# Gate and up of the first 512 columns interleaved per k-unit, quadrants evacuated when complete, down k-units reordered: a Hymba-style block on one Trainium2 core

## The chip, the cores and the metric

The kernel runs on one core of a Trainium2 chip. The metric is the device time of one execution in microseconds (us). Before the change it is 1779.33 us, the median of three executions (1777.89 to 1781.35).

## The reference

The reference is one layer over 256 tokens with D = 2048 and FF = 5632, all in fp32:

```
x = x + 0.5 * swiglu(rms_norm(x, ffn1_norm), w_gate, w_up, w_down)     # ffn1
z = rms_norm(x, mix_norm) @ w_in                                       # 2048 x 5120
y = concat(rms_norm(lru branch of z), rms_norm(short conv branch of z))
x = x + y @ w_out                                                      # the mixer
x = x + 0.5 * swiglu(rms_norm(x, ffn2_norm), ...)                      # ffn2
return rms_norm(x, final_norm)
swiglu(x) = (silu(x @ w_gate) * (x @ w_up)) @ w_down                   # 2048 -> 5632 -> 2048
```

The two swiglu blocks hold most of the work: six weight matrices of 46 MB each.

## The kernel before

**Split products.** [...] A weight unit is 512 rows (a k-unit) by 512 columns, 1 MB. `load` (L155) fetches it from HBM by SyncE's queue (SP) into a raw buffer; `parts_of` (L169) makes hi by two casts on ScalarE (ACT) and lo = raw - hi by one subtraction on VectorE (DVE). `multiply` (L194) then issues 24 matmuls for the 256 tokens (two tiles of 128 tokens, four blocks of 128 rows, three products): first the 16 with the weight's hi, then the 8 with its lo.

**Buffers.** Raw units go through a pool of three buffers. Two further buffers, with the tag "kept", belong to the ffn: a raw unit that is needed for long gets one of those. hi and lo units go through two buffers each, every third one through a further one. [...]

**The norm.** `Norm.turn` (L220) transposes x by PE and writes the gain-scaled result, split, to xT; `squares` sums the squares, `factor` (L237) makes the factor r of each token, and `rows` (L243) spreads r along the free axis by two small matmuls into a bank called pb, copied by DVE to a tile bc.

**The ffn** (`ffn`, L384, called with tag 1 and tag 2). FF is cut into 11 blocks of 512 columns. The first block is done plainly: the gate product over four k-units (in ffn1 by `opening`, L542, with its instructions pinned to the written order, since x has just come from HBM; in ffn2 by `product`, L286), then `norm.factor` and `norm.rows`, and then the up product over the four k-units. Both use the x that is not normalised and apply r behind the sum. Beside the up product DVE and ACT normalise x: per k-unit u, v = hi + lo of xT (`vs`: two tiles v_0 and v_1 with the tag "kept", each for two k-units), v times bc, and v split into the tile x_u; after u = 1 `seven_of` (L308) makes from v_0 four combinations (spare and the quarters of v_0), split into the tiles xs.

The other ten blocks are done two at a time by `seven` (L326), once for gate and once for up: two of the four k-units (rows) by two column blocks by two token tiles are eight products of 128 x 512 x 512, which a scheme of Strassen's kind does with seven, in the banks a, c, e, d; the other two k-units are added plainly (`usual`). The combinations of weights (w11, w12, w22, w21) are made in place by subtractions on DVE (2.29 us each). w11 and w12, needed the longest, are loaded to "kept" buffers:

```python
w11, w12 = get(r0, 0, True), get(r0, 1, True)
```

So in the first `seven` of each ffn these two loads take the buffers of v_0 and v_1. `snap` copies a bank to SBUF by ACT, and four additions at the end of `seven` put the quadrants together; the caller then applies silu or multiplies by the gate.

**The hidden units.** A finished quarter h of 128 tokens x 512 goes on the list `waiting`; `settle` takes it off and calls `turn_hidden` (L397), which transposes it by PE (bank ph), splits it to `hidden[u]` and, where asked, copies the transposed quarter back for `seven_of`. `settle` is called inside the next `seven` of the gate or behind the first k-unit of the down product.

**Down** (`down`, L460, after s = 0, 2 and 4): the hidden units collected so far are multiplied with w_down. Of the four blocks of 512 output columns, blocks 0 and 3 are done by `product`, 1 and 2 together by `seven` with the last two units as its rows; `update` adds half of each to xres. In the product of block 0 the units come in the order of `us`, so the unit m = us[-2] comes before n = us[-1].

The engines run their instructions in the order of the built program; where the program isn't pinned, a scheduler sets that order from the dependencies.

Of the kernel before, what the change touches and what calls it, by code (L numbers as in the profile page):

```python
# [12 lines left out]
AF = mybir.ActivationFunctionType  # L13
ALU = mybir.AluOpType
# [34 lines left out]
def hybrid_block(ctx: ExitStack, tc: tile.TileContext, a: dict, out: bass.AP):  # L49
# [273 lines left out]
    def quad(tile):  # L323
        return tile.rearrange("p (j c) -> p j c", j=UK)

    def seven(w, rows, c0, sf, xs, name, keep, between=None):  # L326


        a, c, e, d = (bank(f"ps_{name}_{n}") for n in "aced")

        def get(u, n, kept=False):
            src = w[u * UK * P : (u + 1) * UK * P, c0 + n * CW : c0 + (n + 1) * CW]
            return load(src, f"{name}_{u}{n}", kept=kept)

        (r0, r1), two = rows, len(xs) > 1
# [6 lines left out]
        def snap(ps, n):  # L342
            s = keep(f"{n}_{name}")
            act.copy(s, ps)
            return s
# [36 lines left out]
        return {(1, 1): u3, (0, 1): u2, (1, 0): a, (0, 0): s1}  # L382

    def ffn(tag, norm, after, opening=None):  # L384
        with tc.tile_pool(name=f"ffn{tag}", bufs=1) as fp:
            extra.append(fp)
            turn_of["hold"] = True
# [27 lines left out]
                    turn_hidden(*waiting.pop(0))  # L415


            if opening:
                Engine.pinned = True
                pg = opening(wg)  # L420
                Engine.pinned = False
                flush()
            else:
                pg = product(wg, 0, range(4), norm.xT.__getitem__, f"g{tag}_0")
                flush()
            norm.factor()
            norm.rows()
            sg = [keep(f"sg{tag}_0_{t}") for t in range(NT)]
            for t in range(NT):
                act.activation(sg[t], pg[t], AF.Silu, scale=norm.r[:, t : t + 1])  # L430
# [4 lines left out]
            bcs = norm.bc.unsqueeze(1).to_broadcast([P, UK, S])  # L435
            xs = []
            for u in range(4):
                x = f32(norm.xT[u])
                dve.tensor_tensor(vs[u], x[:, :, :S], x[:, :, S:], op=ALU.add)
                dve.tensor_tensor(vs[u], vs[u], bcs, op=ALU.mult)  # L440
                xs.append(big(f"x{tag}_{u}"))
                act.copy(xs[u][:, :, :S], vs[u])
                dve.tensor_tensor(xs[u][:, :, S:], vs[u], f32(xs[u][:, :, :S]), op=ALU.subtract)
                if u == 1:
                    pair = [big(f"xs{tag}_{i}") for i in range(2)]
                    sf = seven_of(
                        xs[0], xs[1], {(t, i): vs[i][:, :, t * P : (t + 1) * P] for t in range(NT) for i in range(2)},
                        quad(keep(f"spare{tag}")),
                        [(b[:, :, o : o + P], b[:, :, o + P : o + S]) for b in pair for o in (0, S)],
                    )  # L450
            xs = list(enumerate(xs))[2:]
            pu = product(wu, 0, range(4), norm.xT.__getitem__, f"u{tag}_0")
            for t in range(NT):
                dve.scalar_tensor_tensor(sg[t], pu[t], norm.r[:, t : t + 1], sg[t], op0=ALU.mult, op1=ALU.mult)
                waiting.append((0, t, sg[t], False))
            turn_of["hold"] = False
            if tag == 1:
                prepare()

            def down(last):  # L460
                us = sorted(set(hidden) | {w[0] for w in waiting})

                def update(c, t, ps):
                    xr = xres[:, t, c * CW : (c + 1) * CW]
                    Engine.pinned = last and tag == 2 and c == NC_D - 1
                    dve.scalar_tensor_tensor(xr, ps, 0.5, xr, op0=ALU.mult, op1=ALU.add)
                    if last:
                        after(c, t)

                for c in (0, 3):  # L470
                    end = last and tag == 2 and c == NC_D - 1
                    ps = product(
                        wd, c, us, hidden.get, f"d{tag}_{us[0]}_{c}", end, (lambda i: settle()) if c == 0 else None
                    )
                    for t in range(NT):
                        update(c, t, ps[t])
                    if c == 0:
                        m, n = us[-2:]
# [6 lines left out]
                        q = seven(wd, (m, n), CW, sh, [(u, hidden[u]) for u in us[:-2]], f"d{tag}_{m}", keep)  # L485
                        for c1 in (1, 2):
                            for t in range(NT):
                                update(c1, t, q[t, c1 - 1])
                hidden.clear()
                turned.clear()  # L490

            for s in range(5):
                c0 = CW + 2 * s * CW
                g = seven(wg, (0, 1), c0, sf, xs, f"g{tag}_{s}", keep, settle)
                for q in ((1, 1), (0, 1), (1, 0), (0, 0)):
                    if q == (1, 0):
                        z = keep(f"z{tag}_{s}")
                        act.activation(z, g[q], AF.Silu)
                        g[q] = z
                    else:  # L500
                        act.activation(g[q], g[q], AF.Silu)
                h = seven(wu, (0, 1), c0, sf, xs, f"u{tag}_{s}", keep)
                for t, n in ((1, 1), (0, 1), (1, 0), (0, 0)):
                    dve.tensor_tensor(g[t, n], h[t, n], g[t, n], op=ALU.mult)
                    waiting.append((1 + 2 * s + n, t, g[t, n], s % 2 == 0))
                if s % 2 == 0:
                    down(s == 4)
            extra.clear()
# [30 lines left out]

    n1 = Norm("n1", vec["ffn1_norm"])  # L540

    def opening(wg):  # L542

        ps = [bank(f"ps_g1_0_{t}") for t in range(NT)]
        for u in range(KD // UK):
            src = wg[u * UK * P : (u + 1) * UK * P, :CW]
            if u == 0:
                pieces = ((0, 1), (1, 2), (2, 4))
                raw = load(src, "g1_0_0", pieces, lambda i: load_x(1) if i == 1 else None)
                blk = parts_of(raw, "g1_0_0", pieces, lambda i: n1.turn((i,) if i < 2 else (2, 3)))  # L550
            else:
                blk = unit(src, f"g1_0_{u}")
            for j in range(UK):
                begin, end = u == 0 and j == 0, u == KD // UK - 1 and j == UK - 1
                for t in range(NT):
                    yh, yl = stationary(n1.xT[u], t)[j]
                    pe.matmul(ps[t], yh, blk[j][0], start=begin, stop=False)
                    pe.matmul(ps[t], yl, blk[j][0], start=False, stop=False)
                    pe.matmul(ps[t], yh, blk[j][1], start=False, stop=end)
                if j == (u > 0) and u + 1 < NC_D:  # L560
                    if u:
                        load_x(u + 1)
                        n1.squares(u - 1)
                    n1.turn(range(4 * u + 4, 4 * u + 8))
                elif j == 2 and u + 1 == NC_D:
                    n1.squares(u - 1)
                    n1.squares(u)
        return ps

    held = {}  # L570

    def to_mixer(c, t):
# [3 lines left out]
        else:  # L576
            held["nm"].later(c)

    ffn(1, n1, to_mixer, opening)
    nm = held["nm"]  # L580


# [296 lines left out]
```

## Time and profile before

| | |
|---|---|
| median of three executions | 1779.33 us (1777.89 to 1781.35) |
| the profiled execution's own time | 1779.27 us |
| its span, first to last instruction | 1777.3 us |
| mean granted clock of TensorE | 0.994 |
| PE busy | 1744.6 us, 98% |
| DVE busy | 1494.4 us, 84% |
| ACT busy | 1046.8 us, 59% |
| read from HBM | 339.82 MB, 192 GB/s over the span |

A line of the profile that begins with L42 is an instruction recorded by the kernel's own helper, so all of PE, DVE and ACT stand at L42 and are told apart by their tiles. Tiles are named without buffer numbers and without the ffn's tag: ps_g is the bank of the first gate product, ps_u of the first up product, ps_g_a, ps_g_c and so on the banks of a `seven`; raw, hi and lo with _g, _u, _d are a weight's parts for gate, up and down, with _p those of one of the seven products and with _x those of a `usual` one; ph is a transposed h, pb_n the norm's small matmuls. In a timeline each line has the start, the duration, the engine and operation, output <- inputs, the shapes, and in brackets how long the engine was idle before it and which instruction released it. In the list of waits each line has the engine and tile that waited, what it waited for, the sum, the number of times and the longest.

### The profile page before, as it was taken

The numbers are of one execution on the slowest core, as the hardware profiler recorded it, in microseconds if no ns is written. First come the engines' busy times: TensorE is split into PE (matmuls) and PEld (weight loads), VectorE is DVE, ScalarE is ACT, GpSimd is POOL, SyncE is SP. The second block draws the span as 40 slices with busy tenths as digits, with TensorE's granted clock in tenths as the row PEclk, the third lists the DMA queues.
The fourth block names the chain that finished last, engine by engine and source line by source line (L and its number), as shares of the span: only waits on it lengthen the run. The fifth ranks groups of instructions, "written<-read, shape, count | busy, mean of one in ns | idle before, by whom it ended". The sixth has DMA issues, their size and how long they took to land. (4 is left out here: it accounts for less than half of the span.)

```text
span 1777.3 us, 20302 instructions
## 1 busy us (share of the span) xinstructions
PE 1744.6 (98%) x8031; PEld 1441.5 (81%) x8031; DVE 1494.4 (84%) x1221; ACT 1046.8 (59%) x1342; POOL 6.9 (0%) x32
## 2 busy tenths in 40 slices
PE   7999999999999999999999999999999999999998
PEld 5787888888888888888888887887888888888886
DVE  6898989989789888688987667989899887899895
ACT  6565556656465656575765554656566664556664
POOL 1000000000000000000000000000000000000000
PEclk9999999999999999999999999999999999999999
DMA  7366655574566574456565655574566637555743
GB/s 249 132 214 212 213 189 190 190 245 155 186 196 209 172 256 166 145 188 196 175 196 170 209 189 190 190 242 157 192 214 202 209 135 259 189 190 190 257 158 106
DMA packets 173905, 343.24 MB, mean 193 GB/s; under 512 B 5621, under 2 KB 8049, under 8 KB 173681
## 3 DMA queue, kind: packets, MB, share of 16 engines
q1 hardware_dynamic: 173344, 340.82, 57.2%
q8 instruction: 63, 1.03, 0.2%
q10 hardware_dynamic: 144, 1.05, 0.2%
q14 instruction: 34, 0.27, 0.0%
q0 software_dynamic: 320, 0.07, 0.0%
HBM read 339.82 MB, written 2.10 MB: 192 GB/s over the span
## 5 line engine op out<-in xcount | busy, mean ns | idle before, releaser
L42 PE MATMUL ps_in<-xT_nm,hi_in 128*128 128x512 f32 x640 | 224.1, 395 | 0.0
L42 ACT CAST hi_g_p<-raw_g 128x1024 fp32r<-128x1024 f32 x140 | 140.5, 1048 | 123.4 <-DVE raw_g L42 40.9
L42 DVE TENSOR_TENSOR lo_g_p<-raw_g,hi_g_p 128x2048 fp32r<-128x2048 f32 x70 | 159.7, 2287 | 36.0 <-ACT hi_g_p L42 35.5
L42 ACT CAST hi_u_p<-raw_u 128x1024 fp32r<-128x1024 f32 x140 | 141.5, 1049 | 66.3 <-PE ps_u_a L42 25.9
L42 PE MATMUL ps_in<-xT_nm,lo_in 128*128 128x256 f32 x640 | 178.6, 281 | 0.6 <-DVE lo_in L42 0.6
L42 DVE TENSOR_TENSOR lo_u_p<-raw_u,hi_u_p 128x2048 fp32r<-128x2048 f32 x70 | 159.2, 2286 | 22.2 <-ACT hi_u_p L42 22.1
L42 PE MATMUL ps_d<-hi_d,h 128*128 128x512 f32 x704 | 172.2, 396 | 2.8 <-DVE h L42 2.2
L42 PEld LDWEIGHTS ps_d<-hi_d,h 128*128 128x128 f32 x704 | 132.6, 189 | 33.3 <-DVE h L42 3.0
L42 PEld LDWEIGHTS ps_in<-xT_nm,hi_in 128*128 128x128 f32 x640 | 119.8, 187 | 27.1
L42 ACT CAST hi_d<-raw_d 128x1024 fp32r<-128x1024 f32 x88 | 88.0, 1048 | 81.9 <-PE ps_u_d L42 25.3
L42 DVE TENSOR_TENSOR lo_d<-raw_d,hi_d 128x2048 fp32r<-128x2048 f32 x44 | 100.7, 2289 | 31.7 <-ACT hi_d L42 31.7
L42 PEld LDWEIGHTS ps_in<-xT_nm,lo_in 128*128 128x128 f32 x640 | 120.6, 189 | 1.4 <-DVE lo_in L42 1.1
L42 DVE TENSOR_TENSOR lo_in<-raw_in,hi_in 128x2048 fp32r<-128x2048 f32 x40 | 91.4, 2285 | 32.7 <-ACT hi_in L42 32.5
L42 ACT CAST hi_in<-raw_in 128x1024 fp32r<-128x1024 f32 x80 | 81.5, 1049 | 62.1 <-PE ps_in L42 48.8
L42 ACT CAST hi_d_p<-raw_d 128x1024 fp32r<-128x1024 f32 x84 | 84.5, 1048 | 48.2 <-DVE raw_d L42 21.0
L42 DVE TENSOR_TENSOR lo_d_p<-raw_d,hi_d_p 128x2048 fp32r<-128x2048 f32 x42 | 95.5, 2287 | 18.9 <-ACT hi_d_p L42 18.8
L42 ACT CAST hi_g_x<-raw_g 128x1024 fp32r<-128x1024 f32 x80 | 80.8, 1049 | 41.2 <-PE ps_g_c L42 19.9
L42 ACT CAST hi_u_x<-raw_u 128x1024 fp32r<-128x1024 f32 x80 | 80.6, 1049 | 37.3 <-PE ps_u_c L42 25.8
L42 DVE TENSOR_TENSOR raw_u<-raw_u,raw_u 128x2048 f32<-128x2048 f32 x40 | 91.6, 2291 | 9.4 <-DMA raw_u<-in_ffn_w_up_dram 8.7
L42 DVE TENSOR_TENSOR raw_g<-raw_g,raw_g 128x2048 f32<-128x2048 f32 x40 | 91.5, 2287 | 6.4 <-DMA raw_g<-in_ffn_w_gate_dram 5.8
L42 DVE TENSOR_TENSOR lo_g_x<-raw_g,hi_g_x 128x2048 fp32r<-128x2048 f32 x40 | 91.4, 2286 | 3.8 <-ACT hi_g_x L42 3.7
L42 DVE TENSOR_TENSOR lo_u_x<-raw_u,hi_u_x 128x2048 fp32r<-128x2048 f32 x40 | 91.5, 2287 | 3.7 <-ACT hi_u_x L42 3.1
(349 smaller groups left out, 3612.5 us busy)
## 6 DMA issues: line engine op xcount, KB each, us to landing
raw_u<-in_ffn_w_up_dram SPq DMA_DIRECT2D x88, 1024.0 KB, 5.3
raw_d<-in_ffn_w_down_dram SPq DMA_DIRECT2D x88, 1024.0 KB, 5.1
raw_g<-in_ffn_w_gate_dram SPq DMA_DIRECT2D x87, 1024.0 KB, 5.3
raw_in<-in_w_in_dram SPq DMA_DIRECT2D x40, 1024.0 KB, 5.1
raw_o<-in_w_out_dram SPq DMA_DIRECT2D x16, 1024.0 KB, 5.1
xres<-in_x_dram SPq DMA_DIRECT2D x4, 512.0 KB, 8.3
fin<-in_final_norm_dram ACTq DMA_DIRECT2D x1, 1024.0 KB, 4.7
out_dram<-xres SPq DMA_DIRECT2D x4, 256.0 KB, 2.7
```

Source lines behind the costliest of these rows:

```text
L42: ins = getattr(self.engine, name)(*args, **kwargs)
```

## The change

1. The gate and up products of the first 512 columns are done in one loop: for each k-unit its gate part, then its up part, into four banks. `opening` goes; its pinned order is kept in ffn1 for the first two k-units. Inside that loop `norm.factor` comes after up's k-unit 2 (ffn1) or gate's k-unit 2 (ffn2), and `norm.rows` with the first of the normalising after gate's k-unit 3 (ffn1) or up's k-unit 2 (ffn2). silu of the first block and the multiplication by up follow the loop.
2. `seven` takes a callback `done`, and calls it for each quadrant as soon as its last product is issued: (1,1) after product 6, (0,1) after product 2, (1,0) after the last plain product, (0,0) at the end. The callbacks add the parts (`total`) and apply silu (`gate`) or multiply (`up`); in the down product each part is added to xres by an operation of its own. `between` is called before product 5 instead of after its snap.
3. The up callback calls `settle` at quadrant (1,0), so the two quarters of the unit n are transposed before the last product of up. In the product of block 0 and 3 of down the unit n comes before m, and in down's `seven` the two column blocks change places.

In the built program the pb matmuls come after seven of the eight k-unit parts in ffn1 (24 matmuls of the block are left then) and after six in ffn2 (48 are left); before, they came after the four gate parts (96 are left). The number of matmuls is the same. v_0, v_1 and the first w11, w12 have the same two buffers as before.

```diff
-    def seven(w, rows, c0, sf, xs, name, keep, between=None):
+    def seven(w, rows, cols, sf, xs, name, keep, done, between=None):
...
         product_of(4, w11, c, True)
         s5 = snap(c, "s5")
         usual(0, b2, 1, (e, 1, True, not two), (c, 0, False, False))
+        if between:
+            between()
         dve.tensor_tensor(w11, w22, w11, op=ALU.subtract)
         product_of(5, w11, a)
         u2 = snap(a, "u2")
-        if between:
-            between()
...
         product_of(6, w12, a)
         u3 = snap(a, "u3")
+        done(1, 1, e, [u3, s5])
         product_of(2, w22, c)
+        done(0, 1, c, [u2])
...
+        done(1, 0, a, [])
         product_of(1, w21, d)
-        dve.tensor_tensor(u3, u3, s5, op=ALU.add)
-        dve.tensor_tensor(u3, e, u3, op=ALU.add)
-        dve.tensor_tensor(u2, c, u2, op=ALU.add)
-        dve.tensor_tensor(s1, d, s1, op=ALU.add)
-        return {(1, 1): u3, (0, 1): u2, (1, 0): a, (0, 0): s1}
+        done(0, 0, d, [s1])
...
+            ps = {(m, t): bank(f"ps_{m}{tag}_0_{t}") for m in "gu" for t in range(NT)}
+            Engine.pinned = opening
+            for u in range(KD // UK):
+                for m, w in (("g", wg), ("u", wu)):
...
+                    raw = load(src, n)
+                    if opening and u < 2 and m == "u":
+                        load_x(u + 2)
+                    blk = parts_of(raw, n, ((0, 2), (2, 4)), (lambda i: None) if opening else None)
+                    if opening and u < 3 and m == "u":
+                        norm.turn(range(4 * u + 4, 4 * u + 8))
...
+                    multiply([(ps[m, t], stationary(norm.xT[u], t), u == 0, u == 3) for t in range(NT)], blk)
+                    pump(1.5)
+                    if (u, m) == (1, "u"):
+                        Engine.pinned = False
+                        flush()
+                    elif (u, m) == (2, "u") and opening or (u, m) == (2, "g") and not opening:
+                        norm.factor()
+                    elif (u, m) == (3, "g") and opening or (u, m) == (2, "u"):
+                        norm.rows()
+                        normalise(0)
+                    if u == 3:
+                        for k in range(len(xs), len(xs) + 2):
+                            if k < 4:
+                                normalise(k)
...
                     ps = product(
-                        wd, c, us, hidden.get, f"d{tag}_{us[0]}_{c}", end, (lambda i: settle()) if c == 0 else None
+                        wd, c, us[:-2] + [n, m], hidden.get, f"d{tag}_{m}_{c}", end,
+                        (lambda i: settle()) if c == 0 else None,
                     )
...
+                def up(t, n, ps, tiles):
+                    dve.tensor_tensor(sg[t, n], total(ps, tiles), sg[t, n], op=ALU.mult)
+                    if (t, n) == (1, 0):
+                        settle()
+                    waiting.append((1 + 2 * s + n, t, sg[t, n], s % 2 == 0))
```

More of the change, by code (lines that the diff above doesn't have):

```diff
@@ L376, in seven, with ffn @@
             usual(1, a3, 0, (a, 1, False, True), (d, 0, False, False))
+        done(1, 0, a, [])
         product_of(1, w21, d)
-        dve.tensor_tensor(u3, u3, s5, op=ALU.add)
-        dve.tensor_tensor(u3, e, u3, op=ALU.add)
-        dve.tensor_tensor(u2, c, u2, op=ALU.add)
-        dve.tensor_tensor(s1, d, s1, op=ALU.add)
-        return {(1, 1): u3, (0, 1): u2, (1, 0): a, (0, 0): s1}
-    def ffn(tag, norm, after, opening=None):
+        done(0, 0, d, [s1])
+    def ffn(tag, norm, after, opening=False):
         with tc.tile_pool(name=f"ffn{tag}", bufs=1) as fp:
@@ L415, in settle, with normalise @@
                     turn_hidden(*waiting.pop(0))
[L418 to L430, printed above, removed]
             vs = [fp.tile([P, UK, 2, S], F32, tag="kept", name=f"v{tag}_{i}", bufs=2) for i in range(2)]
             vs = [vs[u // 2][:, :, u % 2, :] for u in range(4)]
-            bcs = norm.bc.unsqueeze(1).to_broadcast([P, UK, S])
-            xs = []
-            for u in range(4):
+            xs, sf = [], {}
+            def normalise(u):
+                bcs = norm.bc.unsqueeze(1).to_broadcast([P, UK, S])
                 x = f32(norm.xT[u])
@@ L445, in ffn @@
                     pair = [big(f"xs{tag}_{i}") for i in range(2)]
[L446 to L449, printed above, removed]
-                    )
+                    sf.update(
+                        seven_of(
+                            xs[0], xs[1],
+                            {(t, i): vs[i][:, :, t * P : (t + 1) * P] for t in range(NT) for i in range(2)},
+                            quad(keep(f"spare{tag}")),
+                            [(b[:, :, o : o + P], b[:, :, o + P : o + S]) for b in pair for o in (0, S)],
+                        )
+                    )
@@ L451, in ffn @@
+            for k in range(len(xs), 4):
+                normalise(k)
             xs = list(enumerate(xs))[2:]
-            pu = product(wu, 0, range(4), norm.xT.__getitem__, f"u{tag}_0")
             for t in range(NT):
-                dve.scalar_tensor_tensor(sg[t], pu[t], norm.r[:, t : t + 1], sg[t], op0=ALU.mult, op1=ALU.mult)
-                waiting.append((0, t, sg[t], False))
+                sg = keep(f"sg{tag}_0_{t}")
+                act.activation(sg, ps["g", t], AF.Silu, scale=norm.r[:, t : t + 1])
+                dve.scalar_tensor_tensor(sg, ps["u", t], norm.r[:, t : t + 1], sg, op0=ALU.mult, op1=ALU.mult)
+                waiting.append((0, t, sg, False))
@@ L461, in down, with update @@
                 us = sorted(set(hidden) | {w[0] for w in waiting})
-                def update(c, t, ps):
+                m, n = us[-2:]
+                def update(c, t, *parts):
                     xr = xres[:, t, c * CW : (c + 1) * CW]
-                    Engine.pinned = last and tag == 2 and c == NC_D - 1
-                    dve.scalar_tensor_tensor(xr, ps, 0.5, xr, op0=ALU.mult, op1=ALU.add)
+                    for p in parts:
+                        dve.scalar_tensor_tensor(xr, p, 0.5, xr, op0=ALU.mult, op1=ALU.add)
                     if last:
@@ L484, in down, with add @@
                         )
[L485 to L488, printed above, removed]
+                        got = {}
+                        def add(t, b, ps, tiles):
+                            got[t, b] = [ps] + tiles
+                            if (0, b) in got and (1, b) in got:
+                                for i in range(NT):
+                                    update(2 - b, i, *got[i, b])
+                        seven(wd, (m, n), (2 * CW, CW), sh, [(u, hidden[u]) for u in us[:-2]], f"d{tag}_{m}", keep, add)
                 hidden.clear()
@@ L492, in ffn, with total, gate @@
             for s in range(5):
[L493 to L505, printed above, removed]
+                cs = (CW + 2 * s * CW, 2 * CW + 2 * s * CW)
+                sg = {}
+                def total(ps, tiles):
+                    for p in tiles[1:]:
+                        dve.tensor_tensor(tiles[0], tiles[0], p, op=ALU.add)
+                    if not tiles:
+                        return ps
+                    dve.tensor_tensor(tiles[0], ps, tiles[0], op=ALU.add)
+                    return tiles[0]
+                def gate(t, n, ps, tiles):
+                    g = total(ps, tiles)
+                    sg[t, n] = tiles[0] if tiles else keep(f"z{tag}_{s}")
+                    act.activation(sg[t, n], g, AF.Silu)
+                def up(t, n, ps, tiles):
[3 more added lines that the diff above has]
+                    waiting.append((1 + 2 * s + n, t, sg[t, n], s % 2 == 0))
+                seven(wg, (0, 1), cs, sf, xs, f"g{tag}_{s}", keep, gate, settle)
+                seven(wu, (0, 1), cs, sf, xs, f"u{tag}_{s}", keep, up)
                 if s % 2 == 0:
@@ L540, in hybrid_block @@
     n1 = Norm("n1", vec["ffn1_norm"])
[L542 to L568, printed above, removed]
     held = {}
@@ L577, in to_mixer @@
             held["nm"].later(c)
-    ffn(1, n1, to_mixer, opening)
+    ffn(1, n1, to_mixer, True)
     nm = held["nm"]
```

20 lines of the change are left out of this document (18 added, 2 removed).

## The prediction

> **What bounds the kernel now.** First the page's busy shares, then the waits of PE (columns: engine, tile, what it waited for, total us, times, longest).
>
> ```profile
> PE 1744.6 (98%) x8031; PEld 1441.5 (81%) x8031; DVE 1494.4 (84%) x1221; ACT 1046.8 (59%) x1342; POOL 6.9 (0%) x32
> ```
>
> ```profile
> PE ps_g L42 <- DVE lo_g L42: 5.2, 3, 2.0
> PE pb_n L42 <- DVE diag_n L42: 4.5, 1, 4.5
> ...
> PE ps_u L42 <- DVE lo_u L42: 2.6, 1, 2.6
> ...
> PE ps_d L42 <- DVE h L42: 2.2, 2, 1.1
> PE ps_g_c L42 <- ACT hi_g_p L42: 1.6, 1, 1.6
> ...
> PE ps_d_a L42 <- ACT hi_d_p L42: 0.3, 1, 0.3
> ```
>
> PE is the bound. The change issues the same matmuls, so it can only move PE's idle time and the stretches at half clock; every wait that it aims at is in this list. The first five rows add up to 16.1 us, all at three kinds of place: the opening of ffn1 (ps_g, pb_n, ps_g_c), the opening of ffn2 (ps_u) and the first down of each ffn (ps_d). So I read the timeline there (start, duration, engine, operation, in brackets the idle time before it and its releaser). The opening of ffn1:
>
> ```profile
> 11.80 1.23 DVE L42 TENSOR_TENSOR lo_g<-raw_g,hi_g 128x1024 fp32r<-128x1024 f32 x1 [1.67 <-ACT hi_g L42]
> ...
> 46.64 0.76 PE L42 MATMUL pb_n<-diag_n,ones 128*128 128x128 f32 x2 [4.47 <-DVE diag_n L42]
> 48.62 0.42 DVE L42 COPY bc_n<-pb_n 128x256 f32<-128x256 f32 x1 [0.89 <-PE pb_n L42]
> 61.25 0.68 DVE L42 TENSOR_TENSOR xs<-v,xs 128x512 fp32r<-128x512 f32 x1
> 61.96 3.71 SPq L164 DMA_DIRECT2D raw_g<-in_ffn_w_gate_dram  x3
> 67.22 2.00 ACT L42 CAST hi_g_p<-raw_g 128x1024 fp32r<-128x1024 f32 x2 [6.44 <-DMA raw_g<-in_ffn_w_gate_dram]
> 71.52 0.75 DVE L42 SCALAR_TENSOR_TENSOR sg<-ps_u,r_n,sg 128x512 f32<-128x512 f32 x1
> 72.59 2.11 PE L42 MATMUL ps_g_a<-hi_g_p,x 128*128 128x512 f32 x8
> 77.24 2.13 PE L42 MATMUL ps_g_c<-hi_g_p,xs 128*128 128x512 f32 x8 [1.62 <-ACT hi_g_p L42]
> 95.06 1.98 PE L42 MATMUL ps_g_a<-hi_g_p,xs 128*128 128x512 f32 x8
> ```
>
> Read it as one chain. The row bc_n starts the normalising on DVE; its last operation on the first v buffer (v1_0) is the xs at 61.25, which ends at 61.93; the load of raw_g is issued at 61.96. That is no accident: the first weight block of the first seven (w11) and v1_0 have the same tag, "kept", which has two buffers, so this load cannot start before v1_0 is dead. It lands 5.26 us later (67.22), its cast follows, and g_0_a starts. None of it costs PE time in before, because 96 matmuls of the up product run beside it, from 47 to 72 us.
>
> **The change part by part.** Prices first, from the opening and the first down of ffn2 and the first down of ffn1:
>
> ```profile
> 1082.47 0.38 PE L42 MATMUL pb_n<-diag_n,ones 128*128 128x128 f32 x2
> 1083.76 0.43 DVE L42 COPY bc_n<-pb_n 128x256 f32<-128x256 f32 x1 [0.58 <-PE pb_n L42]
> 1095.25 1.22 DVE L42 TENSOR_TENSOR x<-v,x 128x1024 fp32r<-128x1024 f32 x1
> 1096.39 0.68 DVE L42 TENSOR_TENSOR xs<-v,xs 128x512 fp32r<-128x512 f32 x1
> 1097.16 5.85 SPq L164 DMA_DIRECT2D raw_g<-in_ffn_w_gate_dram  x4
> 1100.46 3.47 PE L42 MATMUL ps_u<-lo_u,xT_n 128*128 128x512 f32 x8 [2.55 <-DVE lo_u L42]
> 1102.42 1.99 ACT L42 CAST hi_g_p<-raw_g 128x1024 fp32r<-128x1024 f32 x2 [6.50 <-DMA raw_g<-in_ffn_w_gate_dram]
> 1109.45 2.01 PE L42 MATMUL ps_g_a<-hi_g_p,x 128*128 128x512 f32 x8
> 1130.40 1.98 PE L42 MATMUL ps_g_a<-hi_g_p,xs 128*128 128x512 f32 x8
> ```
>
> ```profile
> 163.70 1.03 PE L42 MATMUL ph<-ident,u_g 128*128 128x128 f32 x8
> 164.57 0.60 PE L42 MATMUL ph<-ident,z 128*128 128x128 f32 x4
> 168.26 5.05 PE L42 MATMUL ps_d<-hi_d,h 128*128 128x512 f32 x14 [1.08 <-DVE h L42]
> 174.96 1.32 PE L42 MATMUL ps_d<-hi_d,h 128*128 128x512 f32 x5
> ```
>
> ```profile
> 1199.05 1.03 PE L42 MATMUL ph<-ident,u_g 128*128 128x128 f32 x8
> 1206.90 1.98 PE L42 MATMUL ps_d<-lo_d,h 128*128 128x512 f32 x8
> 1208.72 0.63 PE L42 MATMUL ps_d<-hi_d,h 128*128 128x512 f32 x2
> ```
>
> ```profile
> 72.30:95.10 22.80, 21.18 (x96) 16.45 (x95) 22.67 (x27) 17.52 (x22) 0.00 (x0) 1.00 0.33 98
> 163.60:175.00 11.40, 9.98 (x44) 7.61 (x43) 10.30 (x10) 6.49 (x12) 0.00 (x0) 0.85 0.24 90
> 169.00:172.40 3.40, 3.40 (x9) 2.71 (x9) 3.40 (x3) 0.42 (x1) 0.00 (x0) 0.50 0.00 0
> ```
>
> A matmul of 512 columns takes 0.2275 us (8 from 1206.90 to 1208.72), a k-unit of 24 takes 5.46, a transpose 0.109 (8 from 163.70 to 164.57). The last fence is a table by stretches (PE, PEld, DVE, ACT, POOL busy, granted clock, DMA share, GB/s): the clock stands at 0.50 for 3.4 us after the waits for h, which costs 1.7.
>
> 1. *Opening of ffn1: the gaps between k-units go, the cover of the chain goes too.* With gate and up of one k-unit back to back, PE has 11 us per k-unit instead of 5.5, and DVE and ACT keep up: the ps_g waits and the pb_n wait vanish. But in the new order of instructions the pb_n matmul stands behind the gate part of the fourth k-unit, and only up's fourth k-unit (24 matmuls, 5.5 us) comes after it, where 96 came before. When does it run? The last lo_g of the first unit ends at 13.03; 12 matmuls after it end at about 15.8; then six units and 24 transposes: 15.8 + 6 x 5.46 + 24 x 0.109 = 51.2. No load holds this up: two of 1 MB per 11 us, each landing some 5.3 after its issue. The copy of bc_n starts 1.29 later (1082.47 to 1083.76), 52.5. From there v1_0 is free after 13.31 (48.62 to 61.93) plus one operation on sg that DVE now has in between (0.75): 66.6. The load takes 5.26, 71.8; half a cast 1.0; g_0_a starts at 72.9 against 72.59. PE is through with the up part at 57.3: a **new wait of some 15 us** on hi_g_p, behind which all of PE is queued; the loads behind w11 on SP's queue wait with it, but their buffers come free only by later casts, and ACT's and DVE's small operations for lru_lambda, now ahead of the cast, fit into the 5.26. After it the clock is halved for a window (+1.7, between 0 and 3.4), and the next product, on w12 - w11, waits as it does now (the 1.62 above; by lo, subtraction and cast against 12 matmuls about 2). From g_0_a to the row at 95.06 PE has 20.85 of work (22.47 without the 1.62): 72.9 + 20.85 + 1.7 + 2 = 97.4. **+2.4 us** against 95.06, from 0 (normalising and pb_n each a us earlier) to +4.4 (two halved windows).
>
> 2. *Opening of ffn2.* The same: pb_n comes after six units instead of four, 10.9 later, at 1093.4; bc_n 1094.7. Here DVE does the last xs before the x of 1095.25, so v2_0 is free after 13.31 - 1.15 = 12.2: 1106.9. Load 5.35 by its rows with the issue (1097.07 to 1102.42), half a cast 1.0: g_0_a at 1113.3, while PE is free at about 1105: a **new wait of 8.4 us**. Then as above 20.95 + 1.7 + 2: 1137.9 against 1130.40. **+7.5 us**, from 5.5 to 9.5; the 2.55 wait that goes is in it.
>
> 3. *First down of each ffn.* Between the transposes and the row at 174.96 PE has 16 x 0.109 + 25 x 0.2275 = 7.4 of work and takes 11.26; in ffn2 9.67. So 3.8 and 2.2 are lost, to the waits for h and to the halved window at 169. In the new order only the last-finished h is transposed behind the first unit, the other unit (n) is multiplied next, and the eviction of h lies beside it. What is late next is DVE, which is busy 10.30 of 11.40 there: the lo of the second product may come about 1 us late. I take **-2.7 and -1.2**, between -6.0 in all (nothing late) and -1 (the wait moves to lo_d).
>
> 4. *Evacuating each quadrant when complete, one addition per part onto xres, transposing n before the last product.* On the sevens' own tiles the longest wait left in the list is the 0.3 on hi_d_p, so earlier copies can gain little. DVE's number of operations stays. **0, within 1.** The cover is PE's own queue; if DVE fell behind, each late block would cost up to 2.3, the length of one lo.
>
> Sum: 2.4 + 7.5 - 3.9 + 0 = **+6.0**. The profiled run took 1779.27 (span 1777.3 and 2.0 around it), the median is 1779.33, so no correction: **1785.3 us**.
>
> [...]
>
> **The rivals.**
>
> A. *The chain is hidden after all: faster.* If the w11 load does not wait for v1_0, or normalising fits beside the last units, nothing replaces the removed waits. Then g_0_a of ffn1 starts at 57.3 instead of 72.59 and the 1.62 goes too, 16.9; ffn2 gains its 2.55 and a halved window, 4.2; the downs 6: 27 in all, **1752**. It decides at a cover of 13.3 + 5.3 + 1 + 1.3 = 21 us after pb_n: four k-units in hand make it true, and the order has one (ffn1) and two (ffn2). That the issue comes 0.03 us after the last xs speaks against it; for it speaks only that nothing but this one tag ties the load to v1_0.
>
> B. *Gains and losses cancel.* The lower ends: ffn1 0, ffn2 +5.5, the downs -6: **1779**. For it speaks that the 15 us of idle PE replace waits of the same sum, so that the ffn1 end hardly moves; against it that ffn2 has just 4.2 to give. (It is also the case in which the change does less than its list of waits says.)
>
> C. *The waits cost more.* DVE, busy 22.67 of 22.80 us behind g_0_a, cannot make up a late start, and there are two halved windows: +4.4 and +9.5, the downs -1: **1792**.
>
> **How the numbers follow.** The forecast (1781 to 1790) gets 0.58, A 0.08, B 0.22, C 0.12. The range is 1777 to 1792: it takes in B and C's centre and leaves out A and the far ends. About 0.2% (3.6 us) is what measurement can tell from no change. Faster by more: A and the corner of B in which ffn2 loses under 2.4, 0.12. Within: most of B and the low end of the forecast, 0.22. Slower: 0.66.
>
> **What would show it.** PE's waits after: ps_g_a on hi_g_p, about 15 us near 57 to 73 and 8 us near 1105 to 1113, with raw_g issued right behind the last xs; ps_g on lo_g and pb_n gone; ps_d on h gone; a halved clock after both waits. Wrong if raw_g lands before 60 us (A), if the row that now stands at 1130.40 moves by under 5 us (B), or if waits for lo_d take the place of those for h.

## The result and the profile after

| | median | range | executions |
|---|---|---|---|
| before | 1778.36 us | 1775.56 to 1781.35 | 6 |
| after | 1785.92 us | 1784.63 to 1787.57 | 6 |

The ratio is 1.0042, with a 95% interval of 1.0029 to 1.0055: slower by 7.5 us. The forecast was 1785.3, which is 6.0 over a before of 1779.33; the six executions of before have a median 1.0 lower. The profiled execution of after took 1786.55 us, its span is 1784.7, 7.4 longer than that of before.

The waits of PE (TensorE) in after (engine, tile, what it waited for, total us, times, longest):

```profile
PE ps_g_a L42 <- ACT hi_g_p L42: 23.4, 3, 15.0
PE ps_g_c L42 <- ACT hi_g_p L42: 3.9, 2, 2.1
...
PE ps_d_a L42 <- DVE lo_d_p L42: 0.7, 1, 0.7
PE ps_u_c L42 <- DVE lo_u_p L42: 0.5, 1, 0.5
```

The waits that the change aims at (ps_g and ps_u on lo, pb_n, ps_d on h, 14.5 us by their rows in before) are gone from the list. One row takes their place: 23.4 us on hi_g_p, of which 15.0 and 8.2 are the wait for the first cast of the first `seven` in ffn1 and ffn2. The timeline of ffn1's opening in after (start, duration, engine, operation; in brackets the idle time before it):

```profile
50.56 0.38 PE L42 MATMUL pb_n<-diag_n,ones 128*128 128x128 f32 x2
51.85 0.43 DVE L42 COPY bc_n<-pb_n 128x256 f32<-128x256 f32 x1 [0.58 <-PE pb_n L42]
65.14 0.68 DVE L42 TENSOR_TENSOR xs<-v,xs 128x512 fp32r<-128x512 f32 x1
65.84 1.50 SPq L164 DMA_DIRECT2D raw_g<-in_ffn_w_gate_dram  x2
70.96 1.99 ACT L42 CAST hi_g_p<-raw_g 128x1024 fp32r<-128x1024 f32 x2 [1.44 <-DMA raw_g<-in_ffn_w_gate_dram]
72.06 3.78 PE L42 MATMUL ps_g_a<-hi_g_p,x 128*128 128x512 f32 x8 [14.97 <-ACT hi_g_p L42]
78.87 3.54 PE L42 MATMUL ps_g_c<-hi_g_p,xs 128*128 128x512 f32 x8 [2.07 <-ACT hi_g_p L42]
98.10 1.98 PE L42 MATMUL ps_g_a<-hi_g_p,xs 128*128 128x512 f32 x8
```

The load of raw_g is again issued right behind the last xs (65.82 to 65.84), lands 5.1 later, and PE stands for 14.97 us. The same in ffn2, where the last xs ends at 1106.39, raw_g is issued at 1106.47 and PE waits 8.17:

```profile
1092.80 0.38 PE L42 MATMUL pb_n<-diag_n,ones 128*128 128x128 f32 x2
1094.09 0.42 DVE L42 COPY bc_n<-pb_n 128x256 f32<-128x256 f32 x1 [0.58 <-PE pb_n L42]
1104.50 1.89 DVE L42 TENSOR_TENSOR xs<-v,xs 128x512 fp32r<-128x512 f32 x3
1111.60 1.99 ACT L42 CAST hi_g_p<-raw_g 128x1024 fp32r<-128x1024 f32 x2 [4.78 <-DMA raw_g<-in_ffn_w_gate_dram]
1112.70 3.78 PE L42 MATMUL ps_g_a<-hi_g_p,x 128*128 128x512 f32 x8 [8.17 <-ACT hi_g_p L42]
1119.43 3.11 PE L42 MATMUL ps_g_c<-hi_g_p,xs 128*128 128x512 f32 x8 [1.80 <-ACT hi_g_p L42]
1138.49 1.98 PE L42 MATMUL ps_g_a<-hi_g_p,xs 128*128 128x512 f32 x8
```

The first down of ffn1, where before had waits for h between the transposes and the next unit, runs on without a wait (no line has a bracket):

```profile
167.62 0.60 PE L42 MATMUL ph<-ident,z 128*128 128x128 f32 x4
168.05 0.60 PE L42 MATMUL ph<-ident,s_g 128*128 128x128 f32 x4
168.41 3.90 PE L42 MATMUL ps_d<-hi_d,h 128*128 128x512 f32 x16
172.15 1.98 PE L42 MATMUL ps_d<-lo_d,h 128*128 128x512 f32 x8
173.96 3.84 PE L42 MATMUL ps_d<-hi_d,h 128*128 128x512 f32 x16
```

The third unit starts at 173.96, where before it was 174.96, although PE came to the down 3.9 us later.

**The ledger.** The same matmul is taken in both traces (counted per bank), and the difference of its starts, after minus before, is followed through the span: +3.04 where the first `seven` of up starts in ffn1, +0.26 behind the first down, +0.40 at the end of ffn1, -0.62 at the end of the mixer, +8.09 at the same place of ffn2, +6.31 behind its first down, +7.89 one pair of blocks later, +7.38 at the last product. So ffn1's opening cost 3.0, its first down gave 2.8 back, ffn2's opening cost 8.7, its first down gave 1.8 back, and the next pair of blocks in ffn2 cost 1.6. The -1.0 in the mixer has no change in PE's waits behind it (0.7 and 0.6 on lo_in): its matmuls ran at a slightly other pace in the two executions (232.3 and 231.3 us from the first start to the last on ps_in).

### The profile page after: what moved, and what is told of

Same layout as the page of the kernel before. It is cut to its first block, busy times and chain, and to the rows that moved or that the text cites. A ratio compares the mean times of both kernels' runs of the same rounds, so it can differ in the third digit from the quotient of the medians.

```text
span 1784.7 us, 20306 instructions
## 1 busy us (share of the span) xinstructions
PE 1740.5 (98%) x8031; PEld 1439.8 (81%) x8031; DVE 1494.5 (84%) x1228; ACT 1047.0 (59%) x1342; POOL 6.9 (0%) x32
```

## The experiments

**Theory:** the loss sits in the two openings alone, in the chain from pb_n over the normalising, v's buffer and the load of w11 to g_0_a, some 20 us, which after covers with 11 or 5.5 us of matmuls. **Rival 1:** part of the loss comes from evacuating quadrants early or from the order of the downs. **Rival 2:** it isn't the buffer; DVE is the bound from pb_n on. All kernels do the whole computation. Each ratio is to runs of before on the same chip (it is not simply the quotient of the two medians); the median of before there was 1778.36 us for after, 1779.87 for old_open, new_open, rows2 and v_keep, 1779.18 for v_split, vk_rows12, old_vk and evac_only, 1779.34 for vk_rows13 and mix, 1777.92 for rows13_kept and after_again. "ends" is the start of up's first `seven` against before in the profile, for ffn2 less what was there at the end of the mixer. By two profiles of one kernel (last run) it is good to about 1 us.

| run | median us | ratio to before (95%) | ffn1 ends | ffn2 ends |
|---|---|---|---|---|
| after | 1785.92 | 1.0042 (1.0029 to 1.0055) | +3.0 | +8.7 |
| old_open | 1775.73 | 0.9980 (0.9971 to 0.9990) | 0.0 | 0.0 |
| new_open | 1789.60 | 1.0057 (1.0034 to 1.0080) | +2.9 | +7.6 |
| rows2 | 1781.78 | 1.0009 (0.9996 to 1.0021) | +3.9 | +2.1 |
| v_keep | 1778.06 | 0.9991 (0.9981 to 1.0001) | -5.8 | +5.3 |
| v_split | 1783.21 | 1.0027 (1.0016 to 1.0037) | +1.1 | +7.9 |
| vk_rows12 | 1772.28 | 0.9958 (0.9943 to 0.9972) | -6.1 | +1.5 |
| old_vk | 1779.55 | 1.0003 (0.9994 to 1.0013) | -0.9 | +5.1 |
| evac_only | 1780.09 | 0.9999 (0.9988 to 1.0010) | +0.7 | -1.2 |
| vk_rows13 | 1765.46 | 0.9920 (0.9903 to 0.9936) | -4.3 | -3.4 |
| mix | 1768.68 | 0.9945 (0.9930 to 0.9960) | -4.5 | -0.3 |
| rows13_kept | 1771.19 | 0.9962 (0.9951 to 0.9974) | -4.8 | -0.2 |
| after_again | 1786.27 | 1.0041 (1.0028 to 1.0055) | +2.3 | +8.6 |

**old_open and new_open: the two halves of the change apart.**

```diff
 # in outline, not word for word
 # old_open: after, with
-            (the loop over k-units with gate and up)
+            pg = opening(wg) or product(wg, ...)
+            norm.factor()
+            norm.rows()
+            (normalise all four)
+            pu = product(wu, ...)
 # new_open: before, with after's loop over k-units instead of those lines
```

> The changed kernel with the opening of before in both ffns (gate product, pb_n, up product); the new evacuation of quadrants and the new order of the downs stay. Theory 1 (the loss is all in the two openings: late pb_n, then normalising, v's buffer, load of w11): by the two profiles the openings cost 3.0 and 8.7 us and the first downs give back 2.8 and 1.8, so this kernel lies some 4 us under before and 11 to 12 under the changed one: 1774 to 1776 us. Rival (evacuating quadrants early also costs, as the new waits in the second pair of blocks of ffn2 hint, 1.6 us): 1776 to 1778.

> The kernel before with the interleaved opening alone; sevens and downs as before. Theory 1: slower than before by the two openings, 3.0 + 8.7 = 11.7 us, so 1789 to 1791 us, with the waits of 15 and 8 us on hi_g_p. Rival (part of the loss comes from the other two parts): 1785 to 1788.

old_open came to 1775.73, 4.1 under before; new_open to 1789.60, 9.7 over it (11.7 were expected; the interval holds both). Both lie in the ranges of theory 1. new_open has the two long waits of after:

```profile
PE ps_g_a L42 <- ACT hi_g_p L42: 23.2, 2, 14.9
```

The openings carry the loss, and the rest of the change is a gain. In the second pair of blocks of ffn2, where after lost 1.6 us, old_open loses 0.8 and new_open, with the sevens of before, nothing.

**rows2: a longer cover in ffn2.**

```diff
-                    if (u, m) == (1, "u"):
+                    if (u, m) == ((1, "u") if opening else (0, "u")):
                         Engine.pinned = False
                         flush()
-                    elif (u, m) == (2, "u") and opening or (u, m) == (2, "g") and not opening:
+                    if (u, m) == ((2, "u") if opening else (1, "g")):
                         norm.factor()
-                    elif (u, m) == (3, "g") and opening or (u, m) == (2, "u"):
+                    elif (u, m) == ((3, "g") if opening else (1, "u")):
                         norm.rows()
```

> The changed kernel, in ffn2 alone the norm's factor, its pb_n matmuls and the normalising are brought forward by one k-unit part each: pb_n after four of the eight parts (96 matmuls left) as before, instead of six. If the length of the cover behind pb_n decides, the 8.2 us wait on hi_g_p in ffn2 goes, and so does the half clock behind it: 9 to 11 us faster than the changed kernel, 1775 to 1777 us; ffn1 unchanged with its 15 us wait. If interleaving itself holds up g_0_a (shared buffers of gate and up), the wait stays and the time is within 3 us of the changed kernel.

ffn2 ends 6.6 us earlier than in after, not 9 to 11: 1781.78. The 8.17 wait shrank to the first row here; the second and third are new:

```profile
1109.11 2.15 PE L42 MATMUL ps_g_a<-hi_g_p,x 128*128 128x512 f32 x8 [1.58 <-ACT hi_g_p L42]
1112.38 1.20 PE L42 MATMUL ps_g_a<-lo_g_p,x 128*128 128x512 f32 x4 [1.12 <-DVE lo_g_p L42]
1115.84 2.67 PE L42 MATMUL ps_g_c<-hi_g_p,xs 128*128 128x512 f32 x8 [2.26 <-ACT hi_g_p L42]
```

Why it fell short is in DVE's queue:

```profile
1084.88 0.38 PE L42 MATMUL pb_n<-diag_n,ones 128*128 128x128 f32 x2
...
1085.29 2.29 DVE L42 TENSOR_TENSOR lo_g<-raw_g,hi_g 128x2048 fp32r<-128x2048 f32 x1 [3.22 <-PE pb_n L42]
1087.50 0.28 DVE L42 TENSOR_SCALAR diag_n<-ident,r_n 128x128 f32<-128x128 f32 x1
...
1088.36 0.42 DVE L42 COPY bc_n<-pb_n 128x256 f32<-128x256 f32 x1 [0.58 <-PE pb_n L42]
```

A lo_g of 2.29 us stands ahead of the second diag_n, so bc_n comes 3.48 behind pb_n instead of 1.29, and a lo_u of 2.28 lies inside the normalising. From pb_n to g_0_a are 24.23 us here against 19.90 in ffn2 of after. A longer cover has more lo parts in it, and DVE makes them too.

**v_keep and v_split: the buffer, and the size of the operations.**

```diff
 # v_keep: v in eight small tiles; v_split: the same operations, v in the kept buffers
-                dve.tensor_tensor(vs[u], x[:, :, :S], x[:, :, S:], op=ALU.add)
-                dve.tensor_tensor(vs[u], vs[u], bcs, op=ALU.mult)
+                for t in range(NT):
+                    v = quad(keep(f"v{tag}_{u}_{t}"))      # v_split: vs[u // 2][:, :, u % 2, h]
+                    dve.tensor_tensor(v, xT[:, :, h], xT[:, :, S + t * P : S + (t + 1) * P], op=ALU.add)
+                    dve.tensor_tensor(v, v, bcs, op=ALU.mult)
...
```

> The changed kernel, pb_n as late as there, but v lies in eight tiles of the pool keep (one per k-unit and token tile) instead of the two buffers of the tag kept, so that the loads of w11 and w12 need not wait for it; DVE's operations on v are halved in size and doubled in number. Theory 1 (the buffer ties the load to the end of normalising): the load is early, the subtractions for w11 and w12 go into DVE's 7 us of idle time before pb_n, the waits on hi_g_p shrink to that for x and xs; 12 to 20 us faster than the changed kernel, 1766 to 1774 us. Rival (DVE is the bound from pb_n on, and the load only fills time that DVE needs anyway): within 4 us of the changed kernel, 1782 to 1787 us, with waits on x or xs in place of those on hi_g_p.

> The changed kernel with v in its two kept buffers as there, only DVE's operations on v cut by token tile as in the run v_keep. In the built order all operations on the first v buffer now come ahead of those that finish x_2 and x_3: 15 operations of 0.6 us behind the copy of bc_n instead of 13.9 us. If the buffer ties the load, raw_g is issued some 4 us earlier, g_0_a of ffn1 starts at about 68 us instead of 72 and the wait falls from 15 to 11; ffn2 the same; 5 to 8 us faster than the changed kernel, 1778 to 1781 us. If cutting the operations were what helped in v_keep (not the buffer), this kernel would come near 1778 with no wait on hi_g_p; if DVE alone is the bound, it stays at 1785.

v_keep: 1778.06, between the two theories. The wait of 15 us in ffn1 is gone, and PE waits for the normalised x itself instead. PE's timeline in v_keep:

```profile
58.42 0.49 PE L42 MATMUL ps_g_a<-hi_g_p,x 128*128 128x512 f32 x1 [1.54 <-ACT x L42]
59.57 2.31 PE L42 MATMUL ps_g_a<-hi_g_p,x 128*128 128x512 f32 x7 [0.66 <-DVE x L42]
...
71.16 1.52 PE L42 MATMUL ps_g_e<-hi_g_x,x 128*128 128x512 f32 x2 [2.85 <-ACT x L42]
```

g_0_a starts 13.6 us earlier than in after (58.42 against 72.06), but of that only 8.9 are left where ffn1's opening ends; in ffn2, 3.4 of 8.4. Both theories hold one after the other: the buffer is the first limit, DVE the second. In ffn1 DVE had idled 6.98 us before its diag_n in after; v_keep puts the first two subtractions for w11 and w12 ahead of it (first after, then v_keep):

```profile
50.98 0.29 DVE L42 TENSOR_SCALAR diag_n<-ident,r_n 128x128 f32<-128x128 f32 x1 [6.98 <-PE pb_n L42]
```

```profile
47.56 4.62 DVE L42 TENSOR_TENSOR raw_g<-raw_g,raw_g 128x2048 f32<-128x2048 f32 x2
52.10 0.28 DVE L42 TENSOR_SCALAR diag_n<-ident,r_n 128x128 f32<-128x128 f32 x1
```

In ffn2 of v_keep these two subtractions start at 1088.46 and 1090.99, behind pb_n (1085.65). That fits ffn1 gaining more than ffn2; no run tests it alone. v_keep does one thing more than free the buffer: in after all additions v = hi + lo are done ahead of bc_n, in v_keep half of them (four of 0.7 us) stand behind it in each opening. So a part of DVE's lateness is of the edit's own making.

v_split, whose additions all stay ahead of bc_n as in after, shows the tie alone. It came to 1783.21, over its range of 1778 to 1781. In ffn1 its release comes only 2.1 us earlier, not 4: from the start of bc_n's copy (52.30) to the end of the last xs (63.68) are 11.4 us against 14.0, and the copy itself is 0.45 later. The load and g_0_a follow:

```profile
61.80 1.88 DVE L42 TENSOR_TENSOR xs<-v,xs 128x512 fp32r<-128x512 f32 x3
...
63.71 4.64 SPq L164 DMA_DIRECT2D raw_g<-in_ffn_w_gate_dram  x2
...
69.02 1.04 ACT L42 CAST hi_g_p<-raw_g 128x1024 fp32r<-128x1024 f32 x1 [2.27 <-DMA raw_g<-in_ffn_w_gate_dram]
...
70.11 2.50 PE L42 MATMUL ps_g_a<-hi_g_p,x 128*128 128x512 f32 x5 [12.54 <-ACT hi_g_p L42]
```

v free 2.1 us earlier, issue 2.13 earlier, g_0_a 1.95 earlier (72.06 to 70.11), ffn1 ends 2.0 earlier: one for one. Cutting the operations gives 2.0 in ffn1 and 0.8 in ffn2 where v_keep gains 8.9 and 3.4, so it is not the main thing that helped v_keep.

**old_vk: the buffer where the cover is long.** old_open with v_keep's edit.

> old_open (the opening of before, 96 matmuls behind pb_n) with v outside the kept buffers. If the tie only matters where the cover is short, little changes: g_0_a had no wait in before; the 1.6 to 2.1 us wait of g_c on hi_g_p may go: 1772 to 1776 us. If the tie also holds the opening of before back, 5 us or more faster than old_open: 1768 to 1771.

1779.55, a miss in the other direction: ffn2 ends 5.1 later than in before, and PE has a wait there that old_open hasn't:

```profile
PE ps_g_a L42 <- DVE lo_g_p L42: 4.4, 1, 4.4
```

The load and the first cast of w11 are early (the cast at 1088.25, in old_open at 1099.00), but lo_g_p stands behind all of the normalising in DVE's queue (1104.84, in old_open 1101.03). In this opening all eight additions v = hi + lo, 0.7 us each, come behind bc_n, where old_open had its four of 1.2 done by 1067.3. So the edit took the tie away and loaded DVE behind pb_n with work that had been done long before; this run doesn't show what the tie alone is worth under the long cover. Moving v to other buffers is no gain in itself.

**evac_only: the early evacuation alone.** old_open with the downs' units in the old order and without the call of `settle` in `up` (the place of `between` and the swapped column blocks of down's `seven` stay as in after).

> Before with only the early evacuation of quadrants (done, one addition per part): opening of before, units of the downs in the old order, settle not moved. The first downs keep their waits for h. If the small waits on lo_d_p, hi_g_p and lo_u_p in ffn2 (1.5 us in the changed kernel and in old_open) belong to the evacuation, this kernel is 1.5 us slower than before; if they come of the new order of the downs, it is within 0.5 us of before and shows no such waits.

1780.09 against 1779.18, ratio 0.9999 (0.9988 to 1.0010): no difference that this measurement can tell. Its profile loses 1.3 us in ffn2's second pair of blocks, 0.5 of it in waits (0.3 on hi_g_p, 0.2 on lo_g_p). The profile of each kernel here with the new sevens loses 0.8 to 1.7 us there, that of new_open none, and none loses any at the same place of ffn1. So in the profiles the loss goes with the evacuation (with `between` and the column blocks moved); why it comes in ffn2 only stays open.

**vk_rows12, vk_rows13, mix, rows13_kept: the place of pb_n.** vk_rows12 is v_keep with rows2's edit in ffn2 and pb_n one part earlier in ffn1; vk_rows13 moves ffn2's pb_n one part further; mix has ffn1 of vk_rows12 and the opening of before in ffn2; rows13_kept is vk_rows13 with v back in the kept buffers, so against after it moves pb_n and what leads up to it (the factor, the last squares in ffn1, and in ffn2 the place where deferred work is flushed):

```diff
-                        norm.squares(u + 1)
+                        if u < 2:
+                            norm.squares(u + 1)
+                        if u == 1:
+                            norm.squares(3)
...
-                    if (u, m) == (1, "u"):
+                    if (u, m) == ((1, "u") if opening else (0, "g")):
...
-                    elif (u, m) == (2, "u") and opening or (u, m) == (2, "g") and not opening:
+                    if (u, m) == ((2, "g") if opening else (0, "u")):
...
-                    elif (u, m) == (3, "g") and opening or (u, m) == (2, "u"):
+                    elif (u, m) == ((2, "u") if opening else (1, "g")):
```

> v_keep (v outside the kept buffers) and the norm brought forward: in ffn2 pb_n after four of the eight k-unit parts as in rows2, in ffn1 after six instead of seven (the squares of the last columns of x come one k-unit earlier). Theory after the first runs: two things are late behind pb_n, the load tied to v's buffer, and DVE's own work (normalising and the lo parts). With the tie gone each k-unit part of cover (5.5 us) takes as much off the waits on x and xs (7.8 us in ffn1, 6.8 in ffn2 in v_keep) until they are gone: 3 to 5 us less in ffn1, 5 to 8 less in ffn2 than v_keep, 1765 to 1770 us. Rival (DVE has no idle time left to move work into): 1776 to 1779.

> vk_rows12 with pb_n of ffn2 one part earlier again: after three of the eight parts, five (27 us of matmuls) left. Theory: behind pb_n DVE has a fixed load (normalising 13 us, the lo parts of the matmuls that are left, 2.3 each, and then the sevens' subtractions), so PE waits until that is done, whatever lies in which buffer; each part moved behind pb_n gives PE 5.5 us more to do and DVE 2.3 more, 3 us net, until PE waits no more. In vk_rows12 the opening of ffn2 ended 1.5 us later than in before: it should end 1.5 us earlier here, 1768 to 1771 us. Rival (the cover is long enough in vk_rows12, what is left comes of DVE's order, which puts lo_g_p behind the normalising): the wait on lo_g_p stays and the time is that of vk_rows12, 1771 to 1774.

> ffn1 as in vk_rows12 (interleaved, v outside the kept buffers, pb_n after six parts), ffn2 with the opening of before (four gate parts, pb_n, four up parts, v in the kept buffers); sevens and downs of the changed kernel in both. By the ledgers of the earlier profiles ffn1's opening ends 6.0 us before that of before and ffn2's neither earlier nor later, and the downs and evacuations give 3 to 4: some 9 to 10 us under before, 1769 to 1771 us. If interleaving helps ffn2 as well once v is out of the way, this is slower than vk_rows12.

> vk_rows13 with v back in the two kept buffers: only the place of pb_n is moved against the changed kernel (ffn1 after six parts instead of seven, ffn2 after three instead of six). By the chain (copy of bc_n 1.3 us behind pb_n, v free 12.2 us after that, load 5.3, half a cast 1.0: 20 us) ffn2 with 27 us of matmuls behind pb_n has no wait on hi_g_p left and ends like vk_rows13 or up to 1 us later; ffn1 with 11 us keeps a wait of 8 to 9 us, its g_0_a starts at about 65 us (72 in the changed kernel, 57 in vk_rows13): 1768 to 1773 us. If v's buffer costs nothing once pb_n is earlier, the time is that of vk_rows13, 1765; if the place of pb_n does not matter by itself, 1780 and over.

vk_rows12 came to 1772.28, short of 1765 to 1770: ffn2 gained 3.8 over v_keep, ffn1 nothing clear. vk_rows13 came to 1765.46, under its range: ffn2 ends 3.4 before that of before. Its ratio to before, 0.9920 (0.9903 to 0.9936), is the lowest here, from four executions between 1762.91 and 1770.25, and its interval overlaps that of mix. mix, 1768.68, lies 0.3 us under its range; by the intervals it can't be told from vk_rows12 either, so these two do not show whether interleaving helps ffn2. rows13_kept is the test of the chain. Its time, 1771.19, is in its range, and so are g_0_a's two numbers: in ffn1 a wait of 8.11 with g_0_a at 65.07, and no wait on g_0_a in ffn2:

```profile
44.99 0.38 PE L42 MATMUL pb_n<-diag_n,ones 128*128 128x128 f32 x2
...
65.07 3.78 PE L42 MATMUL ps_g_a<-hi_g_p,x 128*128 128x512 f32 x8 [8.11 <-ACT hi_g_p L42]
...
1098.04 2.01 PE L42 MATMUL ps_g_a<-hi_g_p,x 128*128 128x512 f32 x8
```

From pb_n to g_0_a are 20.08 us in this ffn1, 19.90 in ffn2 of after (1092.80 to 1112.70) and 21.50 in ffn1 of after: these chains, begun at three different places, are 20 to 21.5 us long. Where lo parts stand in DVE's queue the chain is longer: 24.23 in ffn2 of rows2 with two of them, and in this ffn2 25.16 to the first cast (1070.15 to 1095.31) with three. The kernel is 15.1 us faster than after on the same chip (1786.27 to 1771.19), with no buffer and no operation changed, only the place of two small matmuls and what leads to them and hangs on them.

One expectation of rows13_kept missed: ffn2 should end like vk_rows13 or up to 1 us later, and ends 3.3 later, with a wait of 3.39 on the second product's cast. In ffn1 it is the other way round: g_0_a comes 8.2 us later than in vk_rows13 (65.07 against 56.86), yet the opening ends no later (-4.8 against -4.3). There the freed buffer brings the first product forward and not the end.

**after_again.**

> The changed kernel once more, beside the run above on one chip, for the size of the scatter: 1784 to 1788 us, the wait on hi_g_p of ffn1 within 0.5 us of 15.0 and that of ffn2 within 0.5 of 8.2, since both follow from fixed durations; the pace in the mixer may move by 1 to 2 us.

1786.27, waits of 15.1 and 8.2 as before; the mixer's pace moved by 0.5 us.

## Why the prediction was right

The mechanism was the one forecast, and the likeliest of the four cases came. Step by step, by the profiled executions:

1. *Opening of ffn1, forecast +2.4, measured +3.0.* pb_n came at 50.56 (51.2 forecast), g_0_a at 72.06 (72.9), the wait was 14.97 (15). From g_0_a to the end point it took 26.04 instead of 24.55, so g_0_a came 0.8 earlier and the stretch behind it took 1.5 longer than forecast, and the two errors partly cancel. The term that was too small is the half clock: two windows, not one. The stretches of after, two for each opening, with the granted clock as the third number from the end:

```profile
72.06:75.40 3.34, 3.34 (x8) 2.48 (x8) 3.17 (x8) 0.89 (x1) 0.00 (x0) 0.50 0.27 102
78.90:82.20 3.30, 3.30 (x8) 2.58 (x9) 3.30 (x3) 2.75 (x3) 0.00 (x0) 0.54 0.00 0
1112.70:1116.10 3.40, 3.40 (x8) 2.64 (x9) 2.44 (x2) 0.89 (x1) 0.00 (x0) 0.50 0.25 93
1119.50:1122.30 2.80, 2.80 (x8) 2.19 (x9) 2.80 (x2) 2.72 (x3) 0.00 (x0) 0.63 0.00 0
```

   The second one follows the wait of 2.07 for w12 - w11, the fourth one of 1.80.

2. *Opening of ffn2, forecast +7.5, measured +8.7.* g_0_a at 1112.70 is 1113.32 on before's clock (after was 0.62 ahead at the mixer's end), forecast 1113.3. The rest is again more half clock: 25.79 behind g_0_a, 24.65 forecast.

3. *First downs, forecast -2.7 and -1.2, measured -2.8 and -1.8.* The waits for h are gone in both, worth 4.0 and 2.5 up to the third unit; further on 1.3 are lost again in ffn1, 0.7 of it as the wait on lo_d_p, and 0.7 in ffn2. That a lo part would be late there was the forecast; what makes up the other 1.3 shows in no row of the waits. The sign "waits for lo_d take the place of those for h" so came in part, with 0.7 against the 2.2 of h.

4. *Evacuation, forecast 0 within 1, measured +1.6 in ffn2's second pair of blocks.* Outside its bound in the profile, though evac_only by its times can't be told from before.

The sum of these terms, unrounded, is +8.8; -1.0 in the mixer, -0.5 towards the last down and +0.1 elsewhere, which no step had, make it +7.4. The forecast sum was +6.0. That the time came within 0.6 us of 1785.3 is in part luck: against the forecast the openings cost 1.9 more and the evacuation 1.6 more, the downs gave 0.7 more, what no step had gave 1.4, and the median of before fell by 1.0 from three executions to six.

Rival A (27 us faster) fell where it was weakest: it took the buffer for the only tie. v_keep removes that tie, starts g_0_a near A's 57.3 (58.42) and gains 8.9 and 3.4 us in the openings; what then is late is x itself. Rival B's reason was right for ffn1 alone, where long idle time replaced short waits and the end moved by 3.0. What the prediction held against it decided: ffn2 had little to give and lost 8.7. Rival C counted two halved windows per opening; they came, with +3.0 and +8.7 against its +4.4 and +9.5, but the downs gave 4.6 back and not 1.

## What to carry to other kernels

When waits are removed by bringing work together, look at what the old order hid: here 96 matmuls covered a chain of 20 us (small matmuls, copy, normalising, a buffer's release, a load, a cast), and the new order left 48 and 24 of them behind its start. A chain that the cover hides costs nothing in the profile of before and its whole rest in that of after, so time it from its first instruction to its last, and start it as early as its inputs allow before anything else is moved. Every operation that the scheduler puts inside it (here the lo parts, 2.3 us each) makes it longer. If a load is issued within hundredths of a microsecond behind another tile's last use, look whether the two share a buffer, as they do here by their tag; freeing it helps only up to the next limit, and can move other work into the chain.

## What the runs showed of the hardware

In after the clock stood at 0.50 from 62.12 to 75.77 us (so from 5.0 us after PE ran dry at 57.1), from 79.18 to 82.60, from 1106.60 to 1116.84 and from 1120.25 to 1123.66, and at 1.00 between 75.77 and 79.18 and between 1116.84 and 1120.25. Behind the waits of 14.97, 2.07, 8.17 and 1.80 us that leaves 3.71, 3.42, 4.14 and 3.41 us of matmuls at half clock. From g_0_a to the end point this cost 3.1 us in ffn1 (26.04 - 20.85 - 2.07) and 3.0 in ffn2 (25.79 - 20.95 - 1.80): the half clock cost no more behind a wait of 14.97 than behind one of 8.17, and the stretch behind the wait of 1.80 was as long (3.41) as that behind the wait of 2.07 (3.42). The wait of 1.62 in before (up to 77.24) was followed by none: the stretch 72.30:95.10 is at 1.00.

The 1280 matmuls on ps_in in the mixer, which no edit here touches, took from 229.6 us (evac_only) to 235.3 (vk_rows13) from the first start to the last in the profiled executions, with 232.3 in before, 231.3 in after and 234.8 in new_open. In new_open a wait of 1.7 on lo_in is in it. Differences of 1 us between single profiles of this kernel are read only from waits or ledgers, not from the span.
